# An encoder layer in one program: four token squares move to VectorE, the adaLN weights come in half megabytes, and the planner that writes the instruction order gets other rates, steps and margins

## The chip, the cores and the metric

The kernel runs on one core of a Trainium2 chip. The metric is the device time of one execution in microseconds, as the median of several runs. The engines are named PE (TensorE, matmuls), DVE (VectorE), ACT (ScalarE), POOL (GpSimd) and SP (SyncE, which issues the loads and stores).

## The reference

One pre-norm encoder layer in fp32 with D = 1024, over 1024 prompt tokens and 256 sample tokens that share all weights:

```
mod = c @ w_ada + b_ada                       # adaLN: shift, scale, gate per sequence
h   = rms_norm(x, g) * (1 + scale) + shift
p   = h @ w_in                                # 9 slices of 1024, 16 gate columns, 2 x 1024 merge columns
y_conv = cb * dwconv3(cc * cx) * silu(cz)
h_m    = mlstm(q, k, v, i, f) + mlstm reversed in time     # 4 heads of 256, chunks of 128
y_m    = sigmoid(o) * rms(h_m) * silu(mz)
merged = sig(g0) * (y_conv @ w_proj_conv) + sig(g1) * (y_m @ w_proj_mlstm)
y      = rms_norm(x + gate * (merged @ w_out), final_g)
```

The gates of the mLSTM need running sums and running maxima over the 10 chunks of 128 tokens, per head and direction: that is a chain of small operations, called the recurrence chain below.

## The kernel before

The 1280 tokens are ten chunks c = 0 to 9 of 128 rows. The first half of the program is the product of h with w_in, in which each fp32 operand is split into a high and a low part (wh, wl of a weight; b00H, b00L and so on of the tokens) and three products are summed. Two halves of tokens and two halves of K are combined as in Strassen's scheme, so seven products take the place of eight; their token operands are called b00, b10, b11, t1 to t4 (`both_parts`, L382 for the high part on ACT, L383 for the low part on DVE, and `combine`, L388 on DVE, for sums and differences). One accumulation group is 24 matmuls of 128x320 at L748 into one of three PSUM buffers `acc`; DVE adds it into its result at L665 or ACT copies it at L679, and that frees the buffer. ACT splits weights at L328 and POOL writes their low part at L329; DVE sums of weights are at L621. Silu of a result is L565 (ACT) and L568 (DVE).

**Order.** Nobody writes the order of these instructions by hand. Each operation is told to the class `Board` with an engine, an estimated duration and a step (`op`); `Board.order` then plays all of them against estimated times and, on each engine, takes among those that can start the one with the lowest step. `play` emits the instructions in the order of the played start times, and on the chip every engine then runs its own list strictly in that order. The constants are HANDOFF (time between two engines), LAND and KB_US (latency and rate of a load).

**Beginning** (`beginning`). Eight loads of 1 MB bring the shift and scale columns of w_ada (`load_wa`), each into the buffer that a token operand takes later, so they carry names as b00H or t2L; x follows in loads of 512 KB into t3H, t3L, b11H, b11L, t2H, t2L (c = 0,1; 2,3; 4,5; 6,7; 8; 9). PE runs 32 adaLN matmuls of 4x512 per half (L473); their sums are copied at L485 (DVE and ACT), turned at L489 and become scale and shift (L496 to L499). For the token norm (`norm_x`, four groups: c = 0 to 2, 3 to 4, 5 to 7, 8 to 9) ACT squares every chunk with a running sum (L412), DVE finishes the mean (L414), ACT takes the root (L417), DVE refines it with one Newton step (L420 to L424) and scales the chunk (L429). `turn_x` transposes on PE (L442), and ACT (L447) or DVE (L450) applies scale and shift on the way out of PSUM, half of the pieces each.

**Later.** `gate_inputs` (L919, L920 on DVE, L932 on PE) makes the 16 gate columns; `recurrences` (L976 to L1140) is the recurrence chain. Its helper `then` tells the board one operation after another and raises the step by 2 at each PE link. The PE links are L1044, L1046, L1064, L1081, L1082 and L1114; L1090 to L1111 run on DVE between the last two, and the exponentials L1137 on ACT end it. `by_tokens` (L878) turns finished slices with five transposes each. After these come the mLSTM sweeps and the merge, in a second play of the board.

Of the kernel before, what the change touches and what calls it, by code (L numbers as in the profile page):

```python
# [40 lines left out]
class Board:  # L41
# [4 lines left out]
    SOON, AHEAD = .25, 1.5  # L46
# [25 lines left out]
    def op(self, eng, us, f, r=(), w=(), after=(), low=False):  # L72
        o = self.Op()
        o.eng, o.us, o.f, o.low, o.step, o.n, o.played = eng, us, f, low, self.step, len(self.ops), False
# [20 lines left out]
    def order(self):  # L95

        free = dict.fromkeys(("PE", "DVE", "ACT", "POOL", "SP"), 0.0)
        lanes = 0.0
# [17 lines left out]
        def begin(o):  # L116
            t = free[o.eng]
            if o.low and o.eng == "SP":
                t = max(t, lanes - self.AHEAD)
            for b in o.before:  # L120
                t = max(t, b.end + (0.0 if b.eng == o.eng and b.eng != "SP" else self.HANDOFF))
            for b in o.bufs:
                if not b.held:
                    key = id(b.pool), b.tag
                    if turn[key][0] is not b or not spare[key]:
                        return None
                    t = max(t, min(spare[key]) + self.HANDOFF)
            return t
# [52 lines left out]
def encoder_kernel(  # L181
# [170 lines left out]
    def quarter(nm, pool, tag, first):  # L352
        bs = []
        for part, (wa, xs) in zip("HL", first):
            b = buf(pool, [P, 4 * TH2], F32, tag + part, 1)
            for n in wa:
                wa_at[n] = (lambda b=b: b[:, 0:2 * D]), [(b, 0), (b, 1)]
# [33 lines left out]
    def beginning():  # L391
# [16 lines left out]
        def norm_x(cs):  # L408
            n, s = len(cs), slice(cs[0], cs[-1] + 1)
            sq = [("ssq", c) for c in cs]  # L410
            for c in cs:
                op("ACT", 1.35, lambda c=c: A.activation(junk[:, 0:D], x_at[c][0](), AF.Square, bias=zero[:, 0:1], scale=1.0,  # L412
                                                         accum_out=ssq[:, c:c + 1]), r=[x_at[c][1]], w=[(junk, "x"), ("ssq", c)])
# [18 lines left out]
        def turn_x(cs, kts):  # L432
# [3 lines left out]
            for kt in kts:  # L436
# [9 lines left out]
                if kt % 2 == (cs[0] in (3, 5)):  # L446
                    op("ACT", .2 + .1 * len(cs), lambda px=px, dst=dst, d0=d0, sc=sc, sh=sh: A.activation(  # L447
                        dst[:, d0:d0 + tn], px[:, :tn], AF.Identity, bias=sh, scale=sc), r=[px, "s1"], w=[(dst, int(d0 > 0))])
                else:
                    op("DVE", .17 + .13 * len(cs), lambda px=px, dst=dst, d0=d0, sc=sc, sh=sh: V.tensor_scalar(  # L450
# [17 lines left out]
        pada = [buf(psX, [P, 2, 512], F32, "acc", 3) for _ in range(2)]  # L468
        for kt in range(KT):
            wa, toks = wa_at[kt]  # L470
            for h in range(2):
                for j in range(2):
                    op("PE", .88, lambda h=h, j=j, kt=kt, wa=wa: PE.matmul(  # L473
                        pada[h][0:4, j, :], cz4()[:, kt, :], wa()[:, h * D + j * 512:h * D + (j + 1) * 512],
                        start=kt == 0, stop=kt == KT - 1), r=[(junk, "c"), *toks], w=[(pada[h], j)])
# [44 lines left out]
        for k in range(12):  # L520
            if k in (0, 2, 4):
                corner_load(6 + k)
            if k == 2:
# [8 lines left out]
                board.step = 4  # L532
# [338 lines left out]
    def by_tokens(dst, t, r0, l):  # L871
        vt = new_q()
        for j0, jn in ((0, 3), (3, 2)):
# [6 lines left out]
            op("PE", .11 * jn, turn, r=[t.tok], w=[pv])  # L880
# [24 lines left out]
    def gate_inputs():  # L905
# [18 lines left out]
        def gate_product(*terms):  # L924
            acc = buf(psX, [P, 2, 512], F32, "acc", 3)
            for i, (k0, mv) in enumerate(terms):
# [8 lines left out]
                op("PE", 2.35, mm, r=[w, *MOV_B[mv][0], *MOV_B[mv][1]] + ([acc] if i else []), w=[acc])  # L935
# [21 lines left out]
        op("PE", .7, turn, r=[g.tok for g in gr], w=[pg])  # L957
# [11 lines left out]
    def recurrences():  # L969

        places = [big(), big(), qtile()]
        used = [0] * len(places)

        class Tile:


            def __init__(self, shape):
# [3 lines left out]
                self.i = next(i for i in range(3) if used[i] + n <= (T, T, TH2)[i])  # L981
                self.c = slice(used[self.i], used[self.i] + n)
                used[self.i] += n

# [29 lines left out]
        e, s, z, q, b, Gm = (small(nm) for nm in ("ge", "gs", "gz", "gq", "gb", "gG"))  # L1014
# [101 lines left out]
        mg = new([P, 2, 2, HC])  # L1116
# [714 lines left out]
```

## Time and profile before

| | us |
|---|---|
| runs | 1743.52, 1745.39, 1738.02 (median 1743.52) |
| the profiled execution | 1740.72, span 1738.6 |
| PE busy | 1678.7 (97% of the span) |
| DVE, ACT, POOL busy | 962.9, 607.8, 674.0 |
| mean granted TensorE clock | 0.990 of full speed |

PE is busy nearly all the time, so the span is PE's work plus the short times in which PE waits. Those waits, and the stretches at a lower clock that follow some of them, are found in the timeline of PE and in tables of busy time by stretch. Times are counted from the start of the span.

### The profile page before, as it was taken

To read this page: it belongs to the slowest core of one execution; us is meant where nothing else is said; L and a number is where in the kernel's file an instruction comes from. 1 tells how busy PE (TensorE), PEld (TensorE's weight loads), DVE (VectorE), ACT (ScalarE), POOL (GpSimd) and SP (SyncE) were. 2 spreads that over 40 slices of the span, in tenths; PEclk is the share of its full clock that TensorE was granted. 3 is DMA by queue.
4 is the path that set the end of the run, shared out by engine and by line. 5 is a ranking of instruction groups with operands and counts; after the bars stand their busy time and mean duration, and the time that the engine had idled before them with its cause. 6 is when DMAs were issued, how large, how long until landed. Compare 5 with 4: busy or idle time off the path is not lost.

```text
span 1738.6 us, 27963 instructions
## 1 busy us (share of the span) xinstructions
PE 1678.7 (97%) x10702; PEld 1590.9 (92%) x10702; DVE 962.9 (55%) x1653; ACT 607.8 (35%) x1189; POOL 674.0 (39%) x499
## 2 busy tenths in 40 slices
PE   7889999998999999999999999999999999999997
PEld 1789999897999999999999999999888889998986
DVE  0795443255555555655555765652247777565645
ACT  2753233224554222222222222222246565333322
POOL 0224333233664466766666633333210001323412
PEclk9899999998999999999999999999999999999999
DMA  8224323223553122212222444345878865784631
GB/s 337 78 83 147 119 95 129 60 81 87 159 150 111 52 80 79 68 60 66 70 68 67 144 119 145 106 127 196 294 232 274 267 218 155 229 280 133 219 119 61
DMA packets 216410, 241.88 MB, mean 139 GB/s; under 512 B 12517, under 2 KB 174549, under 8 KB 215253
## 3 DMA queue, kind: packets, MB, share of 16 engines
q1 hardware_dynamic: 216096, 240.05, 43.3%
q8 instruction: 85, 1.39, 0.3%
q14 instruction: 49, 0.39, 0.1%
q10 hardware_dynamic: 180, 0.04, 0.0%
HBM read 171.16 MB, written 68.89 MB: 138 GB/s over the span
## 4 chain that ended last, share of the span: by engine, by line
PE 90%; DVE 5%; issue 2%; DMA 2%; ACT 1%; POOL 0%; ACTq 0%; SPq 0%; DVEq 0%; POOLq 0%
PE acc L748 60%; PE qc L1332 3%; PE u L1350 3%; PE accd L1506 2%; PE accd L1505 2%; PE accd L1507 2%; PE accd L1718 2%; PE accd L1719 2%; PE accd L1717 2%; PE acc L1572 2%; PE acc L1573 2%; PE acc L1574 2%; PE acc L473 2%; PE misc L878 1%; PE misc L1393 1%
## 5 line engine op out<-in xcount | busy, mean ns | idle before, releaser
L665 DVE TENSOR_TENSOR q<-acc,q 128x640 f32<-128x640 f32 x272 | 220.9, 822 | 318.4 <-PE acc L748 314.5
L329 POOL TENSOR_TENSOR wl<-comb,wh 128x512 fp32r<-128x512 f32 x176 | 239.8, 1363 | 308.7 <-ACT wh L328 271.2
L329 POOL TENSOR_TENSOR wl<-raw,wh 128x512 fp32r<-128x512 f32 x136 | 183.4, 1349 | 269.0 <-ACT wh L328 268.5
L748 PE MATMUL acc<-xt,wh 128*128 128x320 f32 x1408 | 264.6, 310 | 0.0
L748 PEld LDWEIGHTS acc<-xt,wh 128*128 128x128 f32 x1408 | 220.6, 188 | 0.4
L328 ACT CAST wh<-comb 128x512 fp32r<-128x512 f32 x176 | 109.0, 620 | 247.1 <-PE acc L748 239.4
L328 ACT CAST wh<-raw 128x512 fp32r<-128x512 f32 x136 | 84.2, 621 | 295.3 <-PE acc L748 223.7
L748 PE MATMUL acc<-xt,wl 128*128 128x320 f32 x704 | 160.4, 309 | 0.0
L1533 POOL TENSOR_TENSOR wl<-raw,wh 128x512 fp32r<-128x512 f32 x28 | 36.2, 1298 | 232.4 <-ACT wh L1532 221.9
L748 PEld LDWEIGHTS acc<-xt,wl 128*128 128x128 f32 x704 | 117.7, 188 | 0.0
L815 POOL TENSOR_TENSOR big<-big,q 128x640 f32<-128x640 f32 x48 | 86.7, 1806 | 47.6 <-DVE q L665 40.5
L621 DVE TENSOR_TENSOR comb<-raw 128x512 f32<-128x512 f32 x88 | 77.7, 883 | 19.4 <-POOL wl L329 14.3
L621 DVE TENSOR_TENSOR comb<-raw,comb 128x512 f32<-128x512 f32 x44 | 43.7, 994 | 79.4 <-POOL wl L329 79.4
L565 ACT ACTIVATE q<-q,zero 128x640 f32<-128x640 f32 x76 | 63.2, 831 | 69.8 <-DVE q L665 68.8
L748 PE MATMUL acc<-t3H,wh 128*128 128x320 f32 x352 | 81.5, 313 | 5.4 <-ACT q L679 5.4
L748 PE MATMUL acc<-b11H,wh 128*128 128x320 f32 x352 | 82.2, 314 | 2.9 <-ACT wh L328 2.9
L748 PE MATMUL acc<-t2L,wh 128*128 128x320 f32 x352 | 80.1, 309 | 3.1 <-DVE t2L L383 3.1
L748 PE MATMUL acc<-b00H,wh 128*128 128x320 f32 x352 | 82.3, 314 | 0.0
L1505 PE MATMUL accd<-y,wh 128*128 128x320 f32 x256 | 79.5, 310 | 2.7 <-DVE og L1483 1.5
L748 PE MATMUL acc<-t3L,wh 128*128 128x320 f32 x352 | 81.3, 313 | 0.0
L748 PE MATMUL acc<-t3H,wl 128*128 128x320 f32 x352 | 81.0, 312 | 0.0
L748 PE MATMUL acc<-t2H,wh 128*128 128x320 f32 x352 | 81.0, 311 | 0.0
(315 smaller groups left out, 4187.4 us busy)
## 6 DMA issues: line engine op xcount, KB each, us to landing
raw<-in_w_in_dram SPq DMA_DIRECT2D x96, 256.0 KB
raw<-in_w_in_dram SPq DMA_DIRECT2D x46, 512.0 KB
th<-th_dr SPq DMA_DIRECT2D x32, 320.0 KB
th_dr<-q SPq DMA_DIRECT2D x28, 320.0 KB
raw<-in_w_proj_conv_dram SPq DMA_DIRECT2D x16, 512.0 KB
k<-kn_dr SPq DMA_DIRECT2D x64, 128.0 KB
raw<-in_w_proj_mlstm_dram SPq DMA_DIRECT2D x16, 512.0 KB
raw<-in_w_out_dram SPq DMA_DIRECT2D x16, 512.0 KB
```

Of the source, the lines that this page charges most:

```text
L328: op("ACT", .63, lambda: A.copy(wh[:], src()), r=r, w=[wh])
L329: op("POOL", 1.4, lambda: G.tensor_tensor(out=wl[:], in0=src(), in1=fp(wh[:]), op=ALU.subtract), r=[*r, wh], w=[wl])
L473: op("PE", .88, lambda h=h, j=j, kt=kt, wa=wa: PE.matmul(pada[h][0:4, j, :], cz4()[:, kt, :], wa()[:, h * D + j * 512:h * D + (j + 1) * 51 ...
L565: A.activation(out, in_, AF.Tanh, bias=zero[:, 0:1], scale=0.5)
L621: op("DVE", .9, lambda: V.tensor_tensor(out=t[:], in0=x(), in1=y(), op=o), r=[x.tok, y.tok], w=[t])
L665: op("DVE", .82, lambda: V.tensor_tensor(out=two(dst()), in0=acc[:, :, 0:TQ], in1=two(t()), op=ALU.add), r=[acc, t.tok], w=[dst.tok])
L748: PE.matmul(acc[:, q, 0:TQ], st_[:, k_, :], m_[:, q * TQ:(q + 1) * TQ], start=k_ == 0 and n == 0, stop=k_ == 3 and n == 2)
L815: op("POOL", 1.65, lambda: G.tensor_tensor(out=dst(), in0=dst(), in1=t(), op=ALU.mult), r=[dst.tok, t.tok], w=[dst.tok])
L1332: PE.matmul(pq[:, 0:HD + 2], qTs[i][:, kd, c * P:(c + 1) * P], C[:, kd, :], start=kd == 0, stop=kd == 1)
L1350: PE.matmul(pu[:, db, 0:HD + 2], k[:, db * P:(db + 1) * P], wv[:], start=True, stop=True)
L1505: PE.matmul(accs[q][:, :TQ], wh, yH, start=kt == 0, stop=False)
L1533: op("POOL", 1.36, lambda wh=wh, wl=wl, src=src: G.tensor_tensor(out=wl[:], in0=src(), in1=fp(wh[:]), op=ALU.subtract), r=[raw, wh], w=[wl])
```

## The change

1. `load_wa` issues two loads of 512 KB in place of one of 1 MB, and an adaLN matmul waits for its half alone.
2. In `norm_x` the chunks c = 1, 3, 5, 7 are squared on DVE by one instruction with a running sum (it writes its products to a third `acc` buffer that nobody reads); c = 0, 2, 4, 6, 8, 9 stay on ACT.
3. In `turn_x`, for the last two groups of chunks, ACT takes three of four pieces and not two; the estimates of both forms are new.
4. Steps of the operands b22, t2 and t3 are lower, so they come sooner.
5. `op` has a margin `slack`, added to HANDOFF where a result comes from another engine: 3 us for each operation of the recurrence chain, 1 us for the transposes of `by_tokens`, 2 us for the gate products. The step no longer rises along the chain, and the chain's scratch needs two tiles `big` and no `q` tile.
6. In the first play loads are planned at 375 KB per us (330 before), and SP starts at 4 us.

```
@@ Board
-    def op(self, eng, us, f, r=(), w=(), after=(), low=False):
+    def op(self, eng, us, f, r=(), w=(), after=(), low=False, slack=0.0):
...
-        lanes = 0.0
+        lanes = free["SP"] = self.FIRST
...
-    t = max(t, b.end + (0.0 if b.eng == o.eng and b.eng != "SP" else self.HANDOFF))
+    t = max(t, b.end + (0.0 if b.eng == o.eng and b.eng != "SP" else self.HANDOFF + o.slack))
@@ beginning
-            ap, toks = wa_at[kt]
-            load(1024, ap, wada[:, kt, 0:2 * D], (), toks)
+            for h, (ap, tok) in enumerate(wa_at[kt]):
+                load(512, ap, wada[:, kt, h * D:(h + 1) * D], (), [tok])
...
+                if c % 2 and c < 8:
+                    op("DVE", 1.3, lambda c=c: V.tensor_tensor_reduce(
+                        out=junk2[:].rearrange("p a b -> p (a b)"), in0=x_at[c][0](), in1=x_at[c][0](), op0=ALU.mult,
+                        op1=ALU.add, scale=1.0, scalar=0.0, accum_out=ssq[:, c:c + 1]), r=[x_at[c][1]], w=[junk2, ("ssq", c)])
...
-                if kt % 2 == (cs[0] in (3, 5)):
+                if kt % 2 == (cs[0] == 3) or cs[0] > 3 and kt % 4 != 3:
...
-                board.step = 4
+                board.step = 3
                 both_parts("b22", B22)
...
-                board.step = 6
+                board.step = 4
                 combine(B11, B22, B11, ALU.add)
                 both_parts("t2", B11)
-                board.step = 7
+                board.step = 5
                 both_parts("t3", B22)
@@ by_tokens, gate_inputs
-            op("PE", .11 * jn, turn, r=[t.tok], w=[pv])
+            op("PE", .12 * jn, turn, r=[t.tok], w=[pv], slack=1.0)
@@ recurrences
-        places = [big(), big(), qtile()]
+        places = [big(), big()]
...
-                if eng == "PE":
-                    board.step += 2
-                op(eng, us, f, r=["pre", *r], w=["pre", *w, *places])
+                op(eng, us, f, r=["pre", *r], w=["pre", *w, *places], slack=3.0)
...
-        mg = new([P, 2, 2, HC])
+        mg = z.longer([P, 2, 2, HC])
@@ the first play
-    board.KB_US = 330.0
+    board.KB_US, board.FIRST = 375.0, 4.0
```

The order that the planner writes moves at the following places. In the changed kernel the same statements have other line numbers: L412 is L418, L485 is L492, L679 is L686, L748 is L755, L1082 is L1096, L1114 is L1128, L1137 is L1152.

ACT at the end of adaLN (comb is the copy of an adaLN sum, t3L holds chunks 2 and 3, rr is the root of the first group of chunks). Before:

```order
L412 ACTIVATE big,ssq<-t3H,zero 128x1024 x2
L485 COPY comb<-acc 4x512
L412 ACTIVATE big,ssq<-t3L,zero 128x1024
L485 COPY comb<-acc 4x512
L412 ACTIVATE big,ssq<-t3L,zero 128x1024
L417 ACTIVATE rr_165<-ssq,zero 128x3
```

With the change:

```order
L418 ACTIVATE big,ssq<-t3H,zero 128x1024
L418 ACTIVATE big,ssq<-t3L,zero 128x1024
L492 COPY comb<-acc 4x512
L329 CAST wh<-raw 128x512 x2
L492 COPY comb<-acc 4x512
L424 ACTIVATE rr_165<-ssq,zero 128x3
```

Both squares that ACT keeps of chunks 0 to 3 now stand ahead of the first copy that waits for PE, and two weight casts stand between the copies.

DVE in the same place with the change, where L414 is the new square and its read of the sum (before, no square stood on DVE, and L485 x2, L414, L496 followed each other):

```order
L414 ISA acc,ssq<-t3H 128x1024
L414 ISA ssq 128x1
L492 COPY comb<-acc 4x512
L414 ISA acc,ssq<-t3L 128x1024
L414 ISA ssq 128x1
L492 COPY comb<-acc 4x512
L421 TENSOR_SCALAR ssq<-ssq 128x3
L503 TENSOR_TENSOR big<-misc,cols 128x32
```

The squares of c = 1 and 3 stand ahead of the copies; those of c = 5 and 7 stand further on, one ahead of the second Newton step and one ahead of the first scale-and-shift of DVE.

PE at the last two links of the recurrence chain (misc is a small PSUM buffer). Before, L1114 stands right behind L1082:

```order
L748 MATMUL acc<-t2H,wl 128x320 x2
L1082 MATMUL misc<-ident,big 1x128
L1114 MATMUL misc<-big,ones 128x160
L748 MATMUL acc<-t3H,wh 128x320 x2
L748 MATMUL acc<-t3L,wh 128x320 x2
```

With the change, around the one and, 35 rows further on, around the other:

```order
L1095 MATMUL misc<-ident,big 128x128
L1096 MATMUL misc<-ident,big 1x128
L755 MATMUL acc<-xt,wh 128x320 x4
L755 MATMUL acc<-xt,wl 128x320 x2
L755 MATMUL acc<-b11H,wh 128x320 x2
...
L755 MATMUL acc<-b10H,wl 128x320 x2
L1128 MATMUL misc<-big,ones 128x160
L755 MATMUL acc<-b10H,wh 128x320 x2
L755 MATMUL acc<-b10L,wh 128x320 x2
```

Three accumulation groups (72 matmuls) now stand between the two links.

ACT at the end of the chain. Before:

```order
L1137 ACTIVATE gcol<-gcol,zero 128x80 x3
L1137 ACTIVATE decay<-decay,zero 128x80
L565 ACTIVATE q<-q,zero 128x640 x2
L679 COPY q<-acc 128x640
```

With the change:

```order
L686 COPY q<-acc 128x640
L329 CAST wh<-comb 128x512
L572 ACTIVATE q<-q,zero 128x640
L329 CAST wh<-raw 128x512
L572 ACTIVATE q<-q,zero 128x640
L329 CAST wh<-comb 128x512
L1152 ACTIVATE gcol<-gcol,zero 128x80 x3
L1152 ACTIVATE decay<-decay,zero 128x80
```

The copy that frees an accumulation buffer now stands ahead of the exponentials.

DVE where the operands b11, t3 and t2 are made (between two adds of finished groups, in the first 130 us). Before:

```order
L383 TENSOR_TENSOR b11L<-xt,b11H 128x640
L388 TENSOR_TENSOR xt<-xt 128x640
L383 TENSOR_TENSOR b11L<-xt,b11H 128x640 x3
L388 TENSOR_TENSOR xt<-xt 128x640 x3
L665 TENSOR_TENSOR q<-acc,big 128x640
L383 TENSOR_TENSOR t3L<-xt,t3H 128x640 x2
```

With the change:

```order
L384 TENSOR_TENSOR b11L<-xt,b11H 128x640 x4
L389 TENSOR_TENSOR xt<-xt 128x640 x4
L384 TENSOR_TENSOR t3L<-xt,t3H 128x640 x4
L672 TENSOR_TENSOR q<-acc,big 128x640
L628 TENSOR_TENSOR comb<-raw 128x512
```

The add that frees an accumulation buffer stands behind twelve operand instructions where it stood behind eight.

## Rows read from the trace of the kernel before

**Rows 1.** The timeline of PE, the instructions ahead of which PE waited, and the first token matmul (at 54.60). Columns: start, duration of the group, engine, line, operation, output and inputs, shapes, count, and in brackets the idle time before it and what ended it.

```profile
10.26 1.01 PE L473 MATMUL acc<-b00H,big 128*4 128x512 f32 x1 [5.17 <-DMA b00H<-in_w_ada_dram]
...
46.94 0.48 PE L442 MATMUL misc<-ident,t3H 128*128 128x128 f32 x1 [5.77 <-DVE t3H L429]
...
54.60 0.88 PE L748 MATMUL acc<-b00H,wh 128*128 128x320 f32 x2
...
112.09 0.56 PE L748 MATMUL acc<-t2L,wh 128*128 128x320 f32 x2 [1.00 <-DVE t2L L383]
...
115.38 0.56 PE L748 MATMUL acc<-t2L,wh 128*128 128x320 f32 x2 [2.14 <-DVE t2L L383]
...
130.69 0.83 PE L748 MATMUL acc<-b11H,wh 128*128 128x320 f32 x2 [2.85 <-ACT wh L328]
...
317.40 0.46 PE L932 MATMUL acc<-b00H,q 128*32 128x320 f32 x2 [2.30 <-DVE q L920]
...
405.55 0.51 PE L1114 MATMUL misc<-big,ones 1*128 1x160 f32 x2 [2.95 <-DVE big L1111]
411.44 0.90 PE L748 MATMUL acc<-t3H,wh 128*128 128x320 f32 x2 [5.39 <-ACT q L679]
...
982.64 0.77 PE L878 MATMUL misc<-ident,q 128*128 128x128 f32 x5 [2.53 <-DVE q L665]
```

**Rows 2.** Busy time by stretch. Columns: stretch (us), its length, then busy us of PE, PEld (PE's weight loads), DVE, ACT and POOL, each with its count of instructions, the granted clock (1.00 is full), the busy share of the DMA engines and what they moved in GB/s.

```profile
45.00:47.00 2.00, 0.06 (x1) 0.06 (x1) 1.96 (x3) 1.00 (x2) 1.33 (x2) 0.61 0.33 65
...
58.00:59.00 1.00, 1.00 (x5) 0.96 (x5) 0.87 (x5) 0.00 (x0) 0.00 (x0) 0.50 0.00 0
59.00:60.00 1.00, 1.00 (x10) 1.00 (x9) 1.00 (x2) 0.71 (x2) 0.00 (x0) 0.94 0.00 0
...
95.00:105.00 10.00, 10.00 (x70) 10.00 (x69) 9.93 (x11) 5.35 (x9) 3.96 (x3) 1.00 0.35 118
...
130.00:135.00 5.00, 3.93 (x16) 3.54 (x17) 4.03 (x5) 3.20 (x5) 2.95 (x2) 0.66 0.83 245
315.00:320.00 5.00, 2.70 (x15) 1.81 (x15) 2.08 (x3) 0.50 (x1) 1.26 (x1) 0.85 0.38 105
...
410.00:415.00 5.00, 3.56 (x13) 3.56 (x14) 3.87 (x5) 2.28 (x5) 2.24 (x2) 0.50 0.71 211
415.00:420.00 5.00, 5.00 (x29) 5.00 (x28) 0.82 (x1) 2.88 (x8) 1.59 (x2) 0.75 0.14 52
980.00:985.00 5.00, 2.47 (x18) 2.36 (x18) 3.26 (x3) 1.38 (x3) 3.20 (x3) 1.00 0.49 157
```

**Rows 3.** The timelines of PE, DVE and ACT at the end of the recurrence chain, with the columns of Rows 1.

```profile
402.32 0.27 PE L1082 MATMUL misc<-ident,big 128*1 128x128 f32 x1
...
402.63 0.23 DVE L1090 COPY big<-misc 1x80 f32<-1x80 f32 x1 [4.79 <-PE misc L1082]
...
405.17 0.23 DVE L1111 TENSOR_TENSOR big<-big 1x80 f32<-1x80 f32 x1
...
409.84 0.83 ACT L565 ACTIVATE q<-q,zero 128x640 f32<-128x640 f32 x1 [0.89 <-DVE q L568]
410.70 0.69 ACT L679 COPY q<-acc 128x640 f32<-128x640 f32 x1
```

**Rows 4.** Busy time by stretch in the first 32 us (columns as in Rows 2), and from the view of the adaLN matmuls' line those of the first load: duration in ns as least, median and most, then the first and last start.

```profile
6.00:7.00 1.00, 0.00 (x0) 0.00 (x0) 0.00 (x0) 0.00 (x0) 0.00 (x0) 1.00 1.00 172
7.00:8.00 1.00, 0.00 (x0) 0.00 (x0) 0.00 (x0) 0.00 (x0) 0.00 (x0) 1.00 0.92 352
8.00:9.00 1.00, 0.00 (x0) 0.00 (x0) 0.00 (x0) 0.00 (x0) 0.00 (x0) 1.00 0.99 401
...
22.00:26.00 4.00, 4.00 (x11) 0.78 (x9) 0.00 (x0) 0.52 (x1) 1.26 (x1) 1.00 1.02 424
...
30.00:32.00 2.00, 2.00 (x6) 0.43 (x5) 0.00 (x0) 1.25 (x3) 0.00 (x0) 1.00 1.02 408
...
L473 PE MATMUL acc<-b00H,big x8: 592/1033/1057, 10.3 to 15.5; 128*4 128x512 f32 x8
```

**Rows 5.** The timelines of ACT, DVE and POOL between the end of adaLN and the first scale-and-shift, with the columns of Rows 1.

```profile
40.61 1.14 ACT L412 ACTIVATE big<-t3L,zero 128x1024 f32<-128x1024 f32 x1
...
41.76 0.28 ACT L417 ACTIVATE rr<-ssq,zero 128x3 f32<-128x3 f32 x1
...
42.67 1.24 DVE L423 TENSOR_SCALAR rt<-rt 128x3 f32<-128x3 f32 x1
43.95 1.18 DVE L424 TENSOR_TENSOR rst<-rt,rr 128x3 f32<-128x3 f32 x1
...
49.24 0.17 DVE L423 TENSOR_SCALAR rt<-rt 128x2 f32<-128x2 f32 x1
...
51.63 1.31 DVE L450 TENSOR_SCALAR xt<-misc,s,shf 128x256 f32<-128x256 f32 x2 [0.57 <-PE misc L442]
...
42.62 3.71 POOL L329 TENSOR_TENSOR wl<-raw,wh 128x512 fp32r<-128x512 f32 x3 [18.75 <-ACT wh L328]
```

**Rows 6.** The timeline of DVE, an operand instruction and an add that frees an accumulation buffer (columns as in Rows 1), and from the view of groups by line and shape the four t3L instructions: busy us in all, mean ns of one, idle time before them.

```profile
53.78 0.83 DVE L383 TENSOR_TENSOR b00L<-xt,b00H 128x640 fp32r<-128x640 f32 x1 [0.76 <-ACT b00H L382]
...
93.98 0.81 DVE L665 TENSOR_TENSOR q<-acc,big 128x640 f32<-128x640 f32 x1
...
L383 DVE TENSOR_TENSOR t3L<-xt,t3H 128x640 fp32r<-128x640 f32 x4 | 4.6, 1188 | 0.0
```

More of the change, by code (lines that the diff above doesn't have):

```diff
@@ L45 @@
     HANDOFF, EACH, ISSUE, LAND, KB_US = .2, .04, .4, 2.2, 230.0
-    SOON, AHEAD = .25, 1.5
+    SOON, AHEAD, FIRST = .25, 1.5, 0.0
     class Buf:
@@ L70, in buf @@
         return b
-    def op(self, eng, us, f, r=(), w=(), after=(), low=False):
+    def op(self, eng, us, f, r=(), w=(), after=(), low=False, slack=0.0):
         o = self.Op()
-        o.eng, o.us, o.f, o.low, o.step, o.n, o.played = eng, us, f, low, self.step, len(self.ops), False
+        o.eng, o.us, o.f, o.low, o.step, o.n, o.played, o.slack = eng, us, f, low, self.step, len(self.ops), False, slack
         o.before = set(after)
@@ L356, in quarter @@
             for n in wa:
-                wa_at[n] = (lambda b=b: b[:, 0:2 * D]), [(b, 0), (b, 1)]
+                wa_at[n] = [((lambda b=b, h=h: b[:, h * D:(h + 1) * D]), (b, h)) for h in range(2)]
             for i, c in enumerate(xs):
@@ L468, in beginning @@
         pada = [buf(psX, [P, 2, 512], F32, "acc", 3) for _ in range(2)]
+        junk2 = buf(psX, [P, 2, 512], F32, "acc", 3)
         for kt in range(KT):
-            wa, toks = wa_at[kt]
-            for h in range(2):
+            for h, (wa, tok) in enumerate(wa_at[kt]):
                 for j in range(2):
                     op("PE", .88, lambda h=h, j=j, kt=kt, wa=wa: PE.matmul(
-                        pada[h][0:4, j, :], cz4()[:, kt, :], wa()[:, h * D + j * 512:h * D + (j + 1) * 512],
-                        start=kt == 0, stop=kt == KT - 1), r=[(junk, "c"), *toks], w=[(pada[h], j)])
+                        pada[h][0:4, j, :], cz4()[:, kt, :], wa()[:, j * 512:(j + 1) * 512],
+                        start=kt == 0, stop=kt == KT - 1), r=[(junk, "c"), tok], w=[(pada[h], j)])
         for c in range(4, NC):
@@ L955, in turn @@
                 PE.transpose(pg[:, c * 32:(c + 1) * 32], gr[c // 5]()[0:32, c % 5 * P:(c % 5 + 1) * P], ident[0:32, 0:32])
-        op("PE", .7, turn, r=[g.tok for g in gr], w=[pg])
+        op("PE", .7, turn, r=[g.tok for g in gr], w=[pg], slack=2.0)
         def spread():
@@ L980, in __init__, with longer @@
                     n *= x
-                self.i = next(i for i in range(3) if used[i] + n <= (T, T, TH2)[i])
+                self.i = next(i for i in range(2) if used[i] + n <= T)
                 self.c = slice(used[self.i], used[self.i] + n)
                 used[self.i] += n
+            def longer(self, shape):
+                t, n = object.__new__(Tile), 1
+                for x in shape[1:]:
+                    n *= x
+                t.shape, t.i, t.c = shape, self.i, slice(self.c.start, self.c.start + n)
+                return t
             def __getitem__(self, i):
@@ L1013, in recurrences @@
         f, i_ = pre_f, pre_i
-        e, s, z, q, b, Gm = (small(nm) for nm in ("ge", "gs", "gz", "gq", "gb", "gG"))
+        e, s, z, q, b = (small(nm) for nm in ("ge", "gs", "gz", "gq", "gb"))
+        Gm = e
         then("DVE", .25)(lambda: V.scalar_tensor_tensor(out=e[:], in0=f, scalar=-1.0, in1=f, op0=ALU.mult, op1=ALU.min))
```

14 lines of the change are left out of this document (8 added, 6 removed).

## The prediction

> **What bounds the kernel now.** I read the shares of busy time first (PE works in 1678.7 us of the span of 1738.6, the table above), then the timeline of PE for every place where it waits, then the busy time by stretch for the granted clock there, and last the other engines' timelines around the longest waits. The waits that this change can touch are in [rows 1]. In each the reader is to see the length and the name behind the arrow: the first load (5.17), the scaled tokens on DVE (5.77), operands on DVE (1.00 and 2.14 at 112 and 115), a weight cast (2.85 at 130.69), the gate columns (2.30 at 317.40), the recurrence chain (2.95 and 5.39, one behind the other, at 405.55 and 411.44) and five transposes (2.53 at 982.64). The second thing to see is the clock. In [rows 2] it falls to 0.50, which is 1.2 GHz of 2.4, during 45 to 47 and comes back during 59 to 60; it is low again in part of 130 to 135 and 315 to 320, and in all of 410 to 415; each time PE had waited 2.3 us or more shortly before. After the 2.53 us at 982 it stayed at 1.00. A long wait so costs twice: at full clock a pass of 320 columns starts every 0.143 us (70 in 10 us), at half every 0.274 (13 in 3.56 us) [rows 2].
>
> **The change part by part.**
>
> *Recurrence chain.* PE waited 2.95 us for DVE's chain L1090 to L1111, which takes from 402.63 to 405.40, since its next link stood right behind the last one; then 5.39 us for the copy L679, which frees an accumulation buffer and stood on ACT behind the exponentials and two silus, ending at 411.39 [rows 1, 3]. Together 8.34 us. From 411.44 to about 417.5 PE then ran at half clock (all of 410 to 415, and 415 to 420 has 0.75, so half of it) [rows 2]: 6.06 us in which 22 passes went at 0.274 where 0.143 would do, 2.9 us. The most that can be had is 11.2 us. In the changed order 72 passes stand between the two links, 72 x 0.143 = 10.3 us, against a chain of 2.8 us plus the five DVE instructions that now stand just ahead of it (each 0.8 us by the add in [rows 6], 4.1 us): 6.9 us, 3.4 to spare. The four earlier links have one to four groups between each other likewise, and the copy now stands ahead of the exponentials. What is late next is the exponentials themselves: behind them on ACT stand weight casts, but two groups ahead of PE's need. I take **-10.5**; the ends are -11.2 and, if half of the wait comes back and the clock still falls, -4.
>
> *Half-megabyte loads.* The queue had moved 0.172 + 0.352 = 0.52 MB by 8.0 us, and a whole MB, with 0.40 per us from there, by 9.3 [rows 4]; PE started at 10.26. The first half is thus there about 1.2 us sooner, and since the adaLN passes at first last 1.03 us and not 0.59 [rows 4], the second half comes in time. After that PE is the slower side, so the end of adaLN moves by **-1.2** (ends: 0, if the eight more issues on SP delay the rest, and -1.3). In [rows 4] x, in loads of 512 KB, goes at 408 GB/s and w_ada, in loads of 1 MB, at 424; 4% of 8 MB is under 1 us on data that PE reaches later anyway, so the size costs nothing here. The Trainium skill, "DMA: Bandwidth & Descriptors", section Bandwidth, says to batch loads to 1 MiB or more; by its table a half megabyte would lie between 138 GB/s (64 KB) and 341 (1 MB), and by an estimate of 280 the last adaLN weights would land near 37 us and the gain of this part would be gone. The row speaks against that.
>
> *Squares and the first norm.* Before, the second square of t3L waited on ACT behind a copy of an adaLN sum and ended at 41.75; the root followed at 41.76, and two Newton steps of DVE, L423 and L424, took 1.24 and 1.18 us beside POOL's three splits (42.62 to 46.33), where L423 alone takes 0.17 [rows 5]. With the change both squares of ACT and both of DVE are done while adaLN still runs. The root then waits for the second copy alone and comes about 2.3 us sooner (1.2 of it the part above), and the first transposes at 43 to 45 in place of 46.94. But a new bound takes over: DVE has two more squares, of c = 5 and 7, between the first scaling and its first scale-and-shift (51.63) [rows 5]. No row shows that instruction. The nearest ones are ACT's square of 1024 columns, 1.14 [rows 5], and DVE's two-operand instruction of 640 columns, 0.83, the least it can be [rows 6]; scaled to 1024 columns this gives 1.33, and I take 1.4 with its read of the sum, and up to 2.5 if it is blocked beside POOL as L424 was. So 2.8 us of new work, against 2.3 us of earlier start and some of the 2.2 us that the blocked Newton step lost: the first L748 moves by the 1.2 us already counted and little more. I take another **-0.7** (ends: +2.2, both squares blocked; -2.7, if the wait of 5.77 becomes so short that the clock does not fall: it came back during 59 to 60 [rows 2], 4.5 us after the first L748 at 54.60 [rows 1], worth 2.0).
>
> *Operands, 60 to 131.* With 9.93 of 10 us DVE is the bound [rows 2]. The number of operand instructions ahead of the last t2L is the same in both orders, so the waits at 112 and 115 (3.1 us in all) are not saved. But the add at 93.98 that frees an accumulation buffer now stands behind twelve operand instructions and not eight, and the four t3L that came in take 4.6 us [rows 6]. The group that needs this buffer started at 95.7, 0.9 us after the add's end. PE will wait 3.7 us there in place of 3.1 later, and the operands then are there. The sum is the same, the clock need not be: after a wait of 2.85 it fell for some 3.4 us (0.66 over 130 to 135) [rows 2], 1.6 us of work. I take **+1.0** (ends: -1.5, +5). The four pieces that move from DVE to ACT fall where DVE waits for PE and count nothing.
>
> *Gates and slices.* At 317.40 the order around the wait is unchanged: **0** (ends 0 and -1.6, the clock's part). At 982.64 the transposes now stand one block of six passes later, 0.9 us: **-0.9** (ends 0 and -2.5). The order from the second play on is the same, and I count nothing there.
>
> Sum: -10.5 - 1.2 - 0.7 + 1.0 - 0.9 = -12.3. The profiled execution took 1740.7 us, so 1728.4; it lies 2.8 us below the median of the runs, 1743.5, on which the sum gives 1731.2. I forecast between them, **1729.5 us**. A measurement of this kernel can tell about 0.5% from no change, 8.7 us: below 1734.8 is faster.
>
> **The rivals.**
>
> *The chain's wait comes back.* The exponentials wait on ACT for DVE's last scalars, the casts behind them come late, and PE waits 4 us and loses its clock. For it: ACT's list is in strict order, and before the change it was just this engine that made the wait of 5.39. Against it: the casts stand two groups ahead. The chain then gives -4, the sum is -5.8: about 1736, within 0.5%.
>
> *DVE eats the beginning.* Both squares are blocked beside POOL (+2.2 instead of -0.7) and the wait at 95 is followed by a longer half clock (+3 and not +1): -7.4, about 1734.5, right on the bound. For it: three neighbours in [rows 5] were blocked. The Trainium skill, "SBUF — State Buffer", section Who interferes with whom, states that a DVE instruction with two SBUF inputs and a GpSimd instruction that reads SBUF exclude each other for a whole instruction; L424 agrees with it, at 1.18 us.
>
> *More than the sum.* No clock falls at 46, 95 and 317 (-2.0, -1.0, -1.6), the chain gives all of 11.2 and the transposes at 982 lose their wait entirely (-1.6 more): about -19, 1722. For it: waits of 2.53 (982) and 2.14 (115) left the clock at 1.00.
>
> *Slower: the half clock stays through the DVE-bound stretch.* The new wait at 95 is the longest of its stretch. If the clock falls there and does not come back while DVE keeps feeding PE in pieces, up to 134, nine groups of 24 passes go at 0.274: 216 x 0.131 = 28 us more, less the 2.85 us of the wait at 130.69. From the sum without the +1.0, -13.3, that makes +12: 1754. It decides against the change from about 47 us of half clock on, which is nearly the whole stretch ((13.3 + 8.7) / 0.48). Against it: at 130 and at 411 the clock came back 3.4 and 6 us after PE had started again [rows 2].
>
> *The change does not do what it says.* Orders are fixed when the program is built, and in them the link and the copy have moved; what is left is that waits only move, which is the first rival.
>
> **How the numbers follow.** The forecast gets 0.62, with 1724 to 1735 of its own; the chain's wait 0.13; DVE in the beginning 0.09; more than the sum 0.12; slower 0.04. Faster: nearly all of the forecast (0.60), all of the fourth case and half of the third, together 0.77. Slower 0.04. The rest, 0.19, is within 0.5%. The range from 1719 to 1738 takes in the -19 on the low side and the first rival on the high side.
>
> **What would show it.** Right: no wait of PE over 1 us between the links of the chain, and a clock of 1.00 there; adaLN starting near 9 us; the first transposes near 44, but the first L748 between 52.5 and 53.5; a new wait of 3 to 4 us near 95 for an add on DVE in place of those at 112 and 115. The forecast is wrong if PE still waits for ACT's copy or casts in the chain, if an adaLN pass waits for its half, or if the clock is at 0.50 for more than 6 us between 95 and 130.

## The result and the profile after

The changed kernel takes 1727.66 us (median of 6 runs, 1724.27 to 1730.24), the kernel before, measured with it, 1741.76 (6 runs, 1738.02 to 1745.39). The ratio is 0.9918 with a 95% interval of 0.9901 to 0.9934: 14 us faster. 1729.5 was forecast, in a range of 1719 to 1738. The profiled execution has a span of 1724.6 us, against 1738.6.

PE's timeline of the changed kernel, at the places of [rows 1] (columns as there; 380.54 and 391.30 are the last two links of the recurrence chain):

```profile
9.05 5.79 PE L480 MATMUL acc<-b00H,big 128*4 128x512 f32 x8 [3.99 <-DMA b00H<-in_w_ada_dram]
...
43.55 0.33 PE L449 MATMUL misc<-ident,t3H 128*128 128x128 f32 x1 [3.60 <-DVE t3H L436]
...
51.70 0.88 PE L755 MATMUL acc<-b00H,wh 128*128 128x320 f32 x2
...
91.14 0.54 PE L755 MATMUL acc<-b00H,wh 128*128 128x320 f32 x2
...
95.34 0.56 PE L755 MATMUL acc<-b10H,wh 128*128 128x320 f32 x2 [0.43 <-DVE q L672]
...
110.97 0.56 PE L755 MATMUL acc<-t2L,wh 128*128 128x320 f32 x2 [2.10 <-DVE t2L L384]
...
126.28 0.57 PE L755 MATMUL acc<-b11H,wh 128*128 128x320 f32 x2 [1.49 <-ACT wh L329]
...
312.19 0.45 PE L939 MATMUL acc<-b00H,q 128*32 128x320 f32 x2 [2.30 <-DVE q L927]
...
380.54 0.27 PE L1096 MATMUL misc<-ident,big 128*1 128x128 f32 x1
...
391.30 0.53 PE L1128 MATMUL misc<-big,ones 1*128 1x160 f32 x2
...
966.48 1.33 PE L885 MATMUL misc<-ident,q 128*128 128x128 f32 x5 [3.48 <-DVE q L672]
...
1208.00 1.90 PE L1365 MATMUL u<-wv,k 128*128 128x258 f32 x4 [1.83 <-DMA th<-th_dr]
```

Three things are to be seen against [rows 1]. The two links of the chain stand 10.8 us apart and neither row has a wait in brackets. The waits at the beginning are shorter (3.99 and 3.60 for 5.17 and 5.77). And the wait ahead of the five transposes has grown, from 2.53 us to 3.48. Busy time by stretch (columns as in [rows 2]):

```profile
50.00:55.00 5.00, 4.99 (x22) 4.40 (x23) 3.48 (x8) 3.67 (x7) 0.00 (x0) 0.55 0.00 0
...
105.00:115.00 10.00, 7.53 (x42) 7.00 (x42) 9.93 (x12) 6.35 (x10) 1.59 (x2) 0.87 0.27 100
...
310.00:315.00 5.00, 2.81 (x20) 2.10 (x21) 2.01 (x3) 0.56 (x2) 1.26 (x1) 1.00 0.39 105
315.00:320.00 5.00, 5.00 (x36) 3.73 (x35) 1.50 (x2) 0.53 (x1) 0.00 (x0) 1.00 0.02 5
...
390.00:400.00 10.00, 10.00 (x68) 9.63 (x67) 5.61 (x12) 4.07 (x9) 3.89 (x3) 1.00 0.29 87
...
965.00:970.00 5.00, 3.52 (x17) 3.52 (x18) 2.25 (x3) 0.80 (x2) 3.30 (x4) 0.66 0.72 220
...
1205.00:1210.00 5.00, 3.17 (x14) 2.57 (x14) 0.95 (x3) 1.57 (x3) 2.54 (x2) 0.82 1.07 366
```

PE is busy all of 390 to 400 at a clock of 1.00: the 10 us at half clock behind the chain are gone. At the gates (312) the wait is the 2.30 us of before, but the clock stays up. At 112, 966, 1208 and 1488 it is the other way round: the clock falls for 3.5 us where it had stayed at 1.00.

| matmul (before, changed) | before | changed | shift | since the row above |
|---|---|---|---|---|
| first adaLN pass | 10.26 | 9.05 | -1.2 | -1.2 |
| first token matmul (L748, L755) | 54.60 | 51.70 | -2.9 | -1.7 |
| b11H after the weight cast | 130.69 | 126.28 | -4.4 | -1.5 |
| gate columns (L932, L939) | 317.40 | 312.19 | -5.2 | -0.8 |
| a matmul early in the second play (L1572, L1587) | 1214.66 | 1198.90 | -15.8 | -10.6 |
| a sweep's matmul (L1332, L1347) | 1259.93 | 1245.56 | -14.4 | +1.4 |
| last wait of the merge (L1718, L1733) | 1705.91 | 1691.90 | -14.0 | +0.4 |

The step of -10.6 holds the chain and the slices: the clock at the gates gave 1.6, the slices took 2.2 back (0.95 of wait and about 1.3 of half clock), and about 11.2 are left for the chain.

### The profile page after: what moved, and what is told of

It reads as the page before. It is cut to its first block, busy times and chain, and to the rows that moved or that the text cites. A ratio compares the mean times of both kernels' runs of the same rounds, so it can differ in the third digit from the quotient of the medians.

```text
span 1724.6 us, 27940 instructions
## 1 busy us (share of the span) xinstructions
PE 1676.9 (97%) x10702; PEld 1591.3 (92%) x10702; DVE 974.6 (57%) x1657; ACT 604.4 (35%) x1185; POOL 679.5 (39%) x499
## 4 chain that ended last, share of the span: by engine, by line
PE 91%; DVE 5%; issue 2%; ACT 1%; DMA 1%; ACTq 0%; SPq 0%; POOL 0%; DVEq 0%; POOLq 0%
PE acc L755 59%; PE u L1365 3%; PE qc L1347 3%; PE accd L1520 2%; PE accd L1521 2%; PE accd L1522 2%; PE accd L1733 2%; PE accd L1734 2%; PE accd L1732 2%; PE acc L1587 2%; PE acc L1588 2%; PE acc L1589 2%; PE acc L480 2%; PE misc L885 1%; PE misc L1408 1%
## 5 line engine op out<-in xcount | busy, mean ns | idle before, releaser
L330 POOL TENSOR_TENSOR wl<-comb,wh 128x512 fp32r<-128x512 f32 x176 | 247.2, 1405 | 304.2 <-ACT wh L329 293.2
L330 POOL TENSOR_TENSOR wl<-raw,wh 128x512 fp32r<-128x512 f32 x136 | 191.6, 1409 | 250.9 <-ACT wh L329 245.1
L755 PE MATMUL acc<-xt,wh 128*128 128x320 f32 x1408 | 264.4, 310 | 0.0
L755 PEld LDWEIGHTS acc<-xt,wh 128*128 128x128 f32 x1408 | 220.6, 188 | 0.1
L755 PE MATMUL acc<-xt,wl 128*128 128x320 f32 x704 | 160.4, 309 | 0.0
L1548 POOL TENSOR_TENSOR wl<-raw,wh 128x512 fp32r<-128x512 f32 x28 | 36.3, 1300 | 233.7 <-ACT wh L1547 233.7
L755 PEld LDWEIGHTS acc<-xt,wl 128*128 128x128 f32 x704 | 117.7, 188 | 0.0
L822 POOL TENSOR_TENSOR big<-big,q 128x640 f32<-128x640 f32 x48 | 78.8, 1641 | 37.1 <-DVE q L672 28.8
L755 PE MATMUL acc<-b00H,wh 128*128 128x320 f32 x352 | 83.0, 316 | 0.0
L755 PE MATMUL acc<-t2L,wh 128*128 128x320 f32 x352 | 80.3, 310 | 2.1 <-DVE t2L L384 2.1
L755 PE MATMUL acc<-b11H,wh 128*128 128x320 f32 x352 | 80.9, 310 | 1.5 <-ACT wh L329 1.5
L755 PE MATMUL acc<-t3H,wh 128*128 128x320 f32 x352 | 81.6, 313 | 0.0
L755 PE MATMUL acc<-t2H,wh 128*128 128x320 f32 x352 | 80.8, 311 | 0.4 <-ACT t2H L383 0.4
L755 PE MATMUL acc<-b10H,wh 128*128 128x320 f32 x352 | 80.6, 309 | 0.4 <-DVE q L672 0.4
L755 PE MATMUL acc<-b11H,wl 128*128 128x320 f32 x352 | 80.1, 308 | 0.9 <-POOL wl L330 0.9
```

What stands on the lines that cost most here:

```text
L330: op("POOL", 1.4, lambda: G.tensor_tensor(out=wl[:], in0=src(), in1=fp(wh[:]), op=ALU.subtract), r=[*r, wh], w=[wl])
L755: PE.matmul(acc[:, q, 0:TQ], st_[:, k_, :], m_[:, q * TQ:(q + 1) * TQ], start=k_ == 0 and n == 0, stop=k_ == 3 and n == 2)
L822: op("POOL", 1.65, lambda: G.tensor_tensor(out=dst(), in0=dst(), in1=t(), op=ALU.mult), r=[dst.tok, t.tok], w=[dst.tok])
L1548: op("POOL", 1.36, lambda wh=wh, wl=wl, src=src: G.tensor_tensor(out=wl[:], in0=src(), in1=fp(wh[:]), op=ALU.subtract), r=[raw, wh], w=[wl])
```

## The experiments

Each edit was made to the kernel before or to the changed kernel. Times of "before" are those measured beside them.

**1. The chain's recording alone** (on the kernel before).

```
+ slack in op and order, FIRST (value 0); mg and Gm reuse older scratch
-        places = [big(), big(), qtile()]      +        places = [big(), big()]
-                if eng == "PE":  board.step += 2
-                op(eng, us, f, r=["pre", *r], w=["pre", *w, *places])
+                op(eng, us, f, r=["pre", *r], w=["pre", *w, *places], slack=3.0)
```

> The kernel before with the margin of 3 us, the unraised steps and the smaller scratch of the recurrence chain alone; beginning, gates and slices as before. Theory (the chain's part is independent of the rest): both waits of PE at 405 and 411 (2.95 and 5.39 us) go, the clock stays at 1.00 from 400 to 420, and the time falls by 11 us (10 to 12). Rival (the order is right, but PE still loses its clock, or another wait of ACT comes in its place): 4 to 8.3 us. All waits before 400 us and the 2.53 us at 982 as before.

1730.84 us beside 1741.51; ratio 0.9934 (0.9919 to 0.9949). Both waits are gone, the other waits are those of [rows 1] to 0.1 us (2.53 at the transposes), and no stretch at half clock lies between 140 and 1200 us. The theory held: -10.7 (8.9 to 14.1 by the interval).

**2. Everything but the chain's recording** (on the changed kernel).

```
-        places = [big(), big()]               +        places = [big(), big(), qtile()]
+                if eng == "PE":  board.step += 2
-                op(..., slack=3.0)            +                op(...)
```

> The changed kernel with the recurrence chain recorded as before (no margin, steps that rise, three scratch tiles), everything else changed. Theory (the parts add): both waits of 2.95 and 5.39 us are back with 10 us at half clock behind them, the time is 11 us above the changed kernel, about 1738.5, which is 3 us below the kernel before. Rival (what the beginning gains is lost at the short waits behind it, as in the beginning alone): 1741, no gain on the kernel before.

1738.33 us beside 1742.22; ratio 0.9976 (0.9967 to 0.9984), 10.7 us above the changed kernel, or 10.2 when each of the two is set against the kernel before measured beside it. PE's timeline has both waits back, as long as before:

```profile
399.14 0.51 PE L1121 MATMUL misc<-big,ones 1*128 1x160 f32 x2 [2.95 <-DVE big L1118]
...
405.04 0.90 PE L755 MATMUL acc<-t3H,wh 128*128 128x320 f32 x2 [5.39 <-ACT q L686]
```

The theory held: the chain is worth 10 to 11 us from either side, and all the rest together about 4.

**3. The beginning alone** (on the kernel before: half-megabyte loads, squares, pieces and steps, at the planner's old rate).

```
+ load_wa, norm_x, turn_x, the lower steps, junk2 as in the change
  board.KB_US = 330.0
```

> The kernel before with the five edits of the beginning (half-megabyte loads, squares on DVE, three of four pieces on ACT, lower steps), and the old planner constants. Theory (the first 130 us gained on their own): the matmul that stood at 130.69 comes 4.4 us earlier and 4 to 6.5 us arrive at the end, where the gates' wait leaves the clock up or takes it down (1.6 us); the chain keeps its 8.3 us of waits. Rival (the beginning gains less, and the planner's new load rate carried the rest): 0 to 2 us.

1741.07 us (10 runs) beside 1741.51; ratio 1.0 (0.9989 to 1.0012). The theory fell. The matmul of 130.69 stands at 128.46, 2.2 us earlier and not 4.4, and the first transposes come at 45.69 and not 43.55. In this profile even the 2.2 us are lost again: the half clock behind 128 lasts 7 us (3.5 before), and the clock falls at 982 and 1224, at waits (2.54 and 1.90) of the length of before.

**4. Half-megabyte loads alone** (on the kernel before).

```
-            load(1024, ap, wada[:, kt, 0:2 * D], (), toks)
+            for h, (ap, tok) in enumerate(wa_at[kt]):
+                load(512, ap, wada[:, kt, h * D:(h + 1) * D], (), [tok])
```

> The kernel before with the half-megabyte adaLN loads alone. Theory: adaLN starts at 9.05 in place of 10.26, everything after it up to the first L748 is 1.2 us earlier, and the time falls by 1 us (0.5 to 1.5, too little for a verdict, so it is read from the trace). Rival (the norm of the first chunks on ACT and DVE is the limit, not adaLN): the first transposes stay at 46.9 and nothing is gained.

1741.36 us beside 1741.51; ratio 0.9998 (0.9989 to 1.0007). The rival was right. PE starts and then waits longer for the first norm:

```profile
9.03 5.80 PE L472 MATMUL acc<-b00H,big 128*4 128x512 f32 x8 [3.94 <-DMA b00H<-in_w_ada_dram]
...
46.98 0.48 PE L442 MATMUL misc<-ident,t3H 128*128 128x128 f32 x1 [7.04 <-DVE t3H L429]
```

ACT's timeline shows why. The planner, which thought the chunks would land later, had put the square of chunk 1 behind the copy that waits for PE, so the last square ends at 41.9 us as before:

```profile
31.28 1.15 ACT L412 ACTIVATE big<-t3H,zero 128x1024 f32<-128x1024 f32 x1 [8.41 <-DMA t3H<-in_x_prompt_dram]
...
37.18 0.57 ACT L484 COPY comb<-acc 4x512 f32<-4x512 f32 x1 [4.66 <-PE acc L472]
37.66 1.14 ACT L412 ACTIVATE big<-t3H,zero 128x1024 f32<-128x1024 f32 x1
```

**5. The planner's old rate** (on the changed kernel).

```
-    board.KB_US, board.FIRST = 375.0, 4.0      +    board.KB_US = 330.0
```

> The changed kernel with the planner's old rate of loads (330 KB per us, start at 0) in the first play. Theory (the rate is what puts the squares ahead of the copies that wait for PE): with it gone the squares of chunks 2 and 3 stand behind the copies again, the first transposes come at 45.7 in place of 43.55, the matmul of 126.28 comes 2.2 us later, and the time rises by 2 us plus or minus what the clock does at the short waits (1.6 us each). Rival (the instructions, not the rate, make the gain): less than 0.7 us later at 126.28.

1728.74 us beside 1741.26; ratio 0.9936 (0.9914 to 0.9958). The first transposes come at 45.96 and the matmul of 126.28 at 128.65, 2.4 us later: the theory held for the beginning. In all the runs show no difference from the changed kernel: the median is 1.1 us above it, but the four runs go from 1724.26 to 1731.88, and the profile is of the fastest. In it the wait ahead of the transposes is shorter and the clock stays up behind it:

```profile
967.05 0.77 PE L885 MATMUL misc<-ident,q 128*128 128x128 f32 x5 [1.68 <-DVE q L672]
```

DVE shows where the changed kernel lost that. Six instructions that stand 9 us ahead of the add that the transposes wait for take 4.42 us at the old rate, as in the kernel before (L1159), and 6.37 in the changed kernel, where POOL works beside them without a gap. In the kernel before, then at the old rate:

```profile
968.10 4.42 DVE L1159 SCALAR_TENSOR_TENSOR big<-big,cols 128x128 f32<-128x128 f32 x6
...
952.48 4.42 DVE L1174 SCALAR_TENSOR_TENSOR big<-big,cols 128x128 f32<-128x128 f32 x6
```

In the changed kernel, on DVE, then on POOL:

```profile
950.56 6.37 DVE L1174 SCALAR_TENSOR_TENSOR big<-big,cols 128x128 f32<-128x128 f32 x6
...
950.79 1.57 POOL L822 TENSOR_TENSOR big<-big,q 128x640 f32<-128x640 f32 x1 [1.55 <-DVE q L672]
952.31 1.34 POOL L330 TENSOR_TENSOR wl<-comb,wh 128x512 fp32r<-128x512 f32 x1
953.62 1.61 POOL L866 TENSOR_TENSOR big<-big,q 128x640 fp32r<-128x640 f32 x1
955.19 1.34 POOL L330 TENSOR_TENSOR wl<-comb,wh 128x512 fp32r<-128x512 f32 x1
```

So the new rate gave 2.4 us at the beginning and took 3.1 at 966 in these two profiles (1.8 of wait, 1.3 of half clock).

**6. All squares on ACT** (on the changed kernel).

```
-                if c % 2 and c < 8:  op("DVE", 1.3, ... tensor_tensor_reduce ...)
                 op("ACT", 1.35, ... Square ...)
```

> The changed kernel with all ten squares on ACT, at the new rate. Theory (order, not the engine of the squares, is what counts): all four first squares stand ahead of the copies, the first transposes come at 43 to 44.5, and DVE, freed of two squares, lets the first L755 start up to 1.5 us sooner; at 126.28 within 1 us, total within 1.5 us of the changed kernel. Rival (DVE's share of the squares makes the gain): first transposes 1.3 to 2.7 us later and the same at 126.28.

1731.63 us beside 1741.26; ratio 0.9948 (0.9932 to 0.9964), 4 us above the changed kernel. First transposes at 45.60, the matmul of 126.28 at 127.83: the theory fell, the rival was right. But it was not the squares' own time: ACT had all four done at 36.5, before the copies. With them there, the planner put two weight casts behind the root and not between the copies, POOL's three splits ran from 40.62 to 44.33 instead of 38.37 to 42.10, and three small DVE instructions (one of adaLN's shift, two of the norm) were blocked beside them:

```profile
40.66 1.26 DVE L499 COPY shf<-big 128x16 f32<-128x16 f32 x1
...
42.03 1.10 DVE L422 TENSOR_TENSOR rt<-rr 128x3 f32<-128x3 f32 x1
43.17 1.18 DVE L423 TENSOR_TENSOR rt<-rt,ssq 128x3 f32<-128x3 f32 x1
```

In the changed kernel three such instructions are blocked as well (0.96, 0.67 and 1.03 us, where they take 0.16 or 0.17 alone), but the first of them ahead of the root. Behind the root, which starts at the same time in both (39.68 and 39.74), the blocking costs 1.4 us there and 3.0 here. Later, ACT's copy of an accumulation buffer ends at 93.38 here, and PE waits for it:

```profile
93.44 0.56 PE L748 MATMUL acc<-b00H,wh 128*128 128x320 f32 x2 [2.66 <-ACT big L679]
```

**7. The squares of chunks 5 and 7 back on ACT** (on the changed kernel).

```
-                if c % 2 and c < 8:           +                if c % 2 and c < 4:
```

> The changed kernel with the squares of chunks 5 and 7 back on ACT; those of 1 and 3 stay on DVE. Theory (the first two squares on DVE pay, since DVE is idle there; the later two stand in the way of DVE's first scale-and-shift at 1.37 us each): the first transposes stay at 43.5, the first L755 comes 1 to 2.5 us before 51.70, the matmul of 126.28 comes 1 us earlier or more; total 0 to 2 us less. Rival (ACT is full there, 12.7 of 15 us from 70 on, and its casts come later): the same or later at 126.28.

1726.70 us beside 1741.06; ratio 0.9916 (0.9901 to 0.9931), within 1 us of the changed kernel. The first L755 stands at 51.89, no sooner than 51.70, and the matmul of 126.28 at 126.25: the theory fell for the later two squares, and the rival was right. (The first transposes stand at 44.19 in this profile, 0.6 later than in the changed kernel; counted from them, the first L755 comes 0.45 us sooner.) DVE is free sooner, but ACT then casts its first b00H at 50.33, behind its own squares, where it had been at 49.99. The bound moved from one engine to the other.

**8. Half of the pieces on DVE again** (on the changed kernel).

```
-                if kt % 2 == (cs[0] == 3) or cs[0] > 3 and kt % 4 != 3:
+                if kt % 2 == (cs[0] in (3, 5)):
```

> The changed kernel with half of the scale-and-shift pieces on DVE as before (four more on DVE, 2.4 us). Theory (this move is what let DVE start its twelve operand instructions at 81.2 and not later, so that the add behind them came in time): they start 2 to 3 us later, PE waits 2 to 3.7 us near 93 for the add L672, and the matmul of 126.28 comes 1.5 to 3 us later. Rival (DVE's start there is set by PE's last transposes, and the pieces cost nothing): within 0.5 us at 126.28 and in all.

1729.65 us beside 1741.26; ratio 0.9935 (0.992 to 0.995), 2 us above the changed kernel; the matmul of 126.28 stands at 127.69, 1.4 us later. That is nearly the expected size, but not by the expected way: DVE's block starts at 81.93, only 0.7 us later, and PE waits for the add behind it no longer than in the changed kernel (0.33 us for 0.43). The t2L that PE then waits for ends on DVE 1.4 us later (112.32 for 110.91): 0.7 from the later start, and 0.7 net because one more operand instruction runs beside POOL (1.93 us, where it takes 0.82 without).

**9. The old steps of b22, t2 and t3** (on the changed kernel).

```
-                board.step = 3 / 4 / 5        +                board.step = 4 / 6 / 7
```

> The changed kernel with the old steps of b22, t2 and t3. Theory (both orders hold the same work ahead of the last t2L): DVE's block is split again by the add, the one wait of 2.10 us at 111 becomes two of 1.0 and 2.1, and the matmul of 126.28 moves by less than 1 us; total within 1 us. Rival (the lower steps made the gain at 126): 1.5 to 3 us later there.

1728.96 us beside 1741.26; ratio 0.9933 (0.9918 to 0.9948). The matmul of 126.28 stands at 125.95, and the wait of 2.10 became 0.44 and 1.29. Up to there the theory held: the steps moved waits and saved none. But that matmul starts when ACT's weight cast is done, and the wait ahead of it is 2.86 us here and 1.49 in the changed kernel. 7 us at half clock follow, and the gate columns come at 314.44 in place of 312.19. Whether the steps or the clock's chance made those 2.2 us is not shown.

**10. A larger margin for the slices** (on the changed kernel).

```
-            op("PE", .12 * jn, turn, r=[t.tok], w=[pv], slack=1.0)
+            op("PE", .12 * jn, turn, r=[t.tok], w=[pv], slack=6.0)
```

> The changed kernel with a margin of 6 us and not 1 us for the transposes of finished slices, which puts those of 966 us 36 passes later. Theory (the wait of 3.48 us there is DVE's lateness behind POOL, and work is there to fill it): wait and half clock go, 4 us less than the changed kernel, so about 1723.5. Rival (the wait moves to an accumulation buffer that the same late DVE instruction frees): within 1 us of the changed kernel.

1720.06 us beside 1741.51; ratio 0.9878 (0.9861 to 0.9894): 7.6 us below the changed kernel where 4 was expected. The transposes start without a wait:

```profile
967.71 0.71 PE L885 MATMUL misc<-ident,q 128*128 128x128 f32 x5
```

No wait of 0.6 us or more is left between 320 and 1190, and the matmul of 1198.90 stands at 1193.55, 5.35 us earlier (0.7 of it stands already at the gates, where the wait is 1.76 us). Most of the rest is the clock, which in this profile stays at 1.00 at 1203 where the changed kernel lost 1.4 us.

**11. Both edits, 7 and 10, together.**

```
  the one line of 7 and the one line of 10
```

> The changed kernel with the slices' margin of 6 us and the squares of 5 and 7 back on ACT. Theory (the two parts are 840 us apart and add): 1 to 2 us below the margin of 6 us alone (1720.1), so about 1718.5. Rival (what the beginning gains is lost to the clock at the short waits behind it): within 0.5 us of it.

1720.43 us beside 1741.06; ratio 0.9877 (0.9861 to 0.9894). Not below edit 10 alone; the rival was right, and edit 7 has nothing to add.

**12. The changed kernel a second time.**

```
  (no edit)
```

> The changed kernel, unedited, for a second profile. Theory (at waits of about 2 us the clock falls in some executions and not in others): the waits of PE are the same to 0.1 us, but at least one of the short stretches at half clock (near 112, 966, 1208 and 1488 us) is absent or another one has come. Rival (each wait has its clock): the same stretches.

One execution, 1728.43 us. The waits are the same to 0.2 us (3.47 at 966.74, 2.30 at 312.44), apart from the one for a load at 1209 (2.28 for 1.83). The four short stretches at half clock are all there, and one more has come, from 127.6 to 131.1 us, behind the wait of 1.48. So the theory held in the one, and the rival in the four: of one kernel's waits, some lower the clock in one execution and not in another.

## Why the prediction was right

**The chain**, five sixths of the forecast, was right in mechanism and size: -10.5 forecast, 10.2 to 10.7 measured by runs from both sides, and about 11.2 in the table above. The copy ahead of the exponentials and the 72 passes between the links did what the order said. The rival in which the exponentials hold the casts did not come: L1152 ran at 396.76 and PE stayed busy.

**Half-megabyte loads** started PE 1.21 us sooner, as forecast (-1.2), and x came no later by more than 0.7 us (ACT's first square at 31.33 for 30.72, while PE reached adaLN's end at 38.9). But the step "so the end of adaLN moves" was taken for a gain of the kernel, and experiment 4 shows it is none by itself: the norm was the limit behind it. By the estimate that the prediction drew from the table of the Trainium skill's "DMA: Bandwidth & Descriptors", section Bandwidth, the last weights would land near 37 us; the trace disagrees, since PE begins with the last load at 35.28 without a wait and ends adaLN near 38.9, 1.2 us sooner than before.

**Squares and the first norm.** The first transposes came at 43.55, inside 43 to 45, and the square on DVE takes 1.23 + 0.14 = 1.37 us, where 1.4 was taken:

```profile
32.55 1.23 DVE L414 CUSTOM_DVE_ANT_0 acc<-t3H 128x1024 f32<-128x1024 f32 x1 [26.85 <-DMA t3H<-in_x_prompt_dram]
33.70 0.14 DVE L414 DVE_READ_ACCUMULATOR2_ANT ssq<- 128x1 f32 x1
```

The first token matmul moved by 2.9 us, not 1.9, and so stands outside the 52.5 to 53.5 that were to show the forecast right. Two terms were mis-sized. The two later squares were taken at 2.8 us on DVE, but they put its first piece only 1.2 us later (from the third scaling's end it comes 5.14 us later and not 3.96), since DVE had waited there 0.36 us for the root and 0.57 for PE. And the prediction reckoned with DVE alone: before, the first cast of b00H stood on ACT behind squares, 0.9 us after DVE's piece (52.17) was there; now it waits for DVE. Before, then after:

```profile
53.03 0.71 ACT L382 CAST b00H<-xt 128x640 fp32r<-128x640 f32 x1
...
49.99 0.72 ACT L383 CAST b00H<-xt 128x640 fp32r<-128x640 f32 x1 [1.53 <-DVE xt L457]
```

The cause, too, is wider than the prediction had it. It gave the gain to the squares; experiments 3, 4, 5 and 6 show that it hangs on the order of squares, copies and casts, which the planner's rate sets. (One reading of the prediction was wrong: [rows 5] show two blocked instructions of DVE, not the three that the second rival counts; the third, a scaling at 45.16, took 1.72 us where the next took 0.74.)

**Operands, 60 to 131.** This step failed: "The group that needs this buffer started at 95.7 ... PE will wait 3.7 us there." PE waited 0.43 us. With three buffers I took the third group on to need the one that DVE holds; but the buffer that ACT's copy had freed in between was taken first:

```profile
90.39 0.68 ACT L686 COPY big<-acc 128x640 f32<-128x640 f32 x1
...
94.48 0.81 DVE L672 TENSOR_TENSOR q<-acc,big 128x640 f32<-128x640 f32 x1
```

The group at 91.14 started without a wait, long before the add, in the buffer that the copy had freed at 91.07; only the next group, at 95.34, needed the one that the add freed at 95.29. The add had a whole group more time (3.5 us) than I gave it. That the copy came in time was close: in experiment 6, where it ended at 93.38, the same group waited 2.66 us. The other assumption of the step, that pieces which move from DVE to ACT "count nothing", was wrong too: experiment 8 puts them at 1.4 us, half of it by one more instruction held beside POOL. In place of +1.0 this stretch gave -1.5. By an estimate 0.9 of that is the clock: the half clock of the start lasted 4.6 us past the first token matmul before and 2.8 us now, and at half clock 0.48 of the time is lost.

**Gates and slices.** At the gates order and wait stayed, as forecast, and the clock gave the 1.6 us of the lower end; that was luck, since the same wait lowers the clock in one profile and not in another (last section). At the slices the step failed: -0.9 forecast, +2.2 measured. The transposes moved back by 0.9 us of work as the order said, but the add ahead of them came 1.9 us later against PE, since POOL's instructions had closed up beside DVE's. I had read the order of PE there and not that of POOL. The wait goes with the planner's rate: at the new rate and a margin of 1 us it is 3.47 to 3.49 us in all seven profiles, at the old rate 2.53 or 2.54 without the margin (four profiles) and 1.68 with it, which is the -0.9 that was forecast. The Trainium skill, "SBUF — State Buffer", section Who interferes with whom, has the rule for it (a DVE instruction with two SBUF inputs and one of POOL that reads SBUF exclude each other), and the six instructions agree: 6.37 us beside POOL, 4.42 with gaps.

**The sum** was off by 1.7 us (-12.3 and -14.0) because the misses offset each other: beginning 3.5 us better than forecast, the clock at 130 and at the gates 2.4 better, the chain 0.7 better, slices 3.1 worse, the second play 1.8 worse (1.4 of it the clock at 1208). The mechanism of the large term was right; that the total came so near is luck in the rest. (In the rival with the half clock the 47 us come to 46 by its own figures.)

What stays open: why the same wait lowers the clock in one kernel or execution and not in another. The margin between edits 10 and 11 and the missing gain of experiment 3 may both lie in it; neither was shown.

## What to carry to other kernels

Where a planner writes the order, a wait that is too long is mended by a margin on that operation, and its price and gain can be read from two rows of the order and the work that now stands between them; the same margin, once more, was worth another 7.6 us here. An estimate in the planner that is a little off (the rate of loads) can undo or carry an edit that looks independent of it, so an edit's gain is measured with the plan it will run under. Before a held buffer is priced, count which groups can take another one.

## What the runs showed of the hardware that was not expected

The clock answers waits of about 2 us now and then. The gates' wait of 2.30 to 2.41 us brought it to half in five of the twelve profiles that have it (the kernel before among them) and left it at 1.00 in seven (the changed kernel in both of its two). The wait ahead of the transposes lowered it in all seven profiles in which it was 3.47 us or more, and in one of four in which it was 2.53 or 2.54. Each fall cost about 1.5 us, so two kernels with the same waits can differ by 3 us in a profile. The runs of one kernel spread by up to 7.4 us (1738.02 to 1745.39 before), and the clock goes along with that: in 19 runs of the kernel before measured together the fastest (1737.53) had a mean granted clock of 0.990 and the slowest (1744.84) of 0.987.
